# Halves of every second up-projection block made by two GpSimd transfers, with 2 raw and 3 low buffers

## The chip, the core and the metric

The kernel runs on one core of one Trainium2 chip. The engines that appear here are PE (TensorE, the matrix engine, with its weight loads shown apart as PEld), DVE (VectorE), ACT (ScalarE), POOL (GpSimd) and SP (SyncE, which here only issues transfers). A "queue" is the engine that issues a transfer: SP, ACT and POOL each issue some. The metric is the device time of one execution in microseconds; lower is better. The kernel before takes 1641.8 us, the median of two runs (1641.42 and 1642.17).

## The reference

One layer of a hybrid encoder works on 256 tokens of width 2048, in float32. A mixer with three branches (latent attention, a short gated convolution, attention into a memory) comes first. The change lies in the feed-forward part behind it:

```python
u = dwconv_centred(rmsnorm(x, ffn_norm) @ w_up, ffn_conv_w)
a, b = jnp.split(u, 2, axis=-1)
x = x + (jax.nn.silu(a) * b) @ w_down
```

`w_up` is 2048 x 11264 and `w_down` 5632 x 2048. A final RMSNorm follows.

## The kernel before

**Two halves for every weight.** Matrix products keep float32 accuracy by splitting each operand in two numbers of the type float32r. The first, `hi`, is the operand rounded to that type; the second, `lo`, is what the rounding lost. A product is then hi times both halves of the activations (512 columns: 256 tokens, high half and low half side by side) plus lo times the high half (256 columns). Weights come from HBM as float32 in blocks of 128 partitions x 2048 (1 MiB), and each block is split on the chip, in three steps:

- `load` (L129): SP issues a transfer of the block into a tile `raw`.
- `halves` (L138): ACT copies `raw` into `hi`, which rounds it.
- `halves` (L139): DVE subtracts, `lo = raw - hi`.

`block` is `load` and then `halves`. The pools have three `raw` buffers, three `hi` and two `lo`.

**Blocks on PE.** `mm` makes one output tile from one block, by `acc`: 15 products with hi (L161), 16 with lo (L163), and the last one with hi (L165). PE goes through the program block by block, about 290 of them.

**Up-projection.** `up(c)` takes two blocks, number 2c for the part `a` and 2c + 1 for the part `b`, both by `block`. Behind the products, `total` adds the two halves of a result (ACT L185, DVE L187), and DVE and ACT apply the norm's factor (L681), the convolution's three taps (L544, L545, L548) and the gate (L686, L687), and split the result f (L194, L195). There are 44 calls, in two groups: 23 before the first down-projection, which takes 32 blocks of 128 x 1408, and 21 before the second, which takes 24 such blocks and a last stage with row-major weights.

**Order.** A scheduler orders the instructions of each engine when the program is built; the order is then fixed, and each engine works its list in order, waiting at semaphores. A transfer into a tile waits until the last reader of the buffer's earlier tile is done. POOL does almost nothing in the up-projection: its one instruction there is the power in `norm_factor` (L228).

Of the kernel before, what the change touches and what calls it, by code (L numbers as in the profile page):

```python
# [12 lines left out]
F32R = mybir.dt.float32r  # L13
I32 = mybir.dt.int32
AF = mybir.ActivationFunctionType
ALU = mybir.AluOpType
# [3 lines left out]
P = 128  # L20
# [16 lines left out]
WB = 2048  # L37
# [39 lines left out]
def tile_kernel(ctx: ExitStack, tc: tile.TileContext, a, out):  # L77
    nc = tc.nc
    ctx.enter_context(nc.allow_low_precision(reason="float32r halves hold float32 exactly"))
    const = ctx.enter_context(tc.tile_pool(name="const", bufs=1))  # L80
    raws = ctx.enter_context(tc.tile_pool(name="raws", bufs=3))
    his = ctx.enter_context(tc.tile_pool(name="his", bufs=3))
    los = ctx.enter_context(tc.tile_pool(name="los", bufs=2))
    slots = ctx.enter_context(tc.tile_pool(name="slots", bufs=54))
    tmp = ctx.enter_context(tc.tile_pool(name="tmp", bufs=2))
    tiny = ctx.enter_context(tc.tile_pool(name="tiny", bufs=2))
# [3 lines left out]
    def f32(ap):  # L90
        return ap.bitcast(F32)
# [4 lines left out]
    def half(t, i):  # L96
        return t[:, i * T : (i + 1) * T]

    def temp(name):
        tag, bufs = {"hl": ("hl", 2), "t": ("t", 3), "s": ("s", 2), "sq": ("sq", 3)}.get(name, ("w", 8))  # L100
        return tmp.tile([P, T], F32, tag=tag, name=name, bufs=bufs)
# [22 lines left out]
    def load(src, n=WB, pieces=1):  # L124
        raw = raws.tile([P, WB], F32, tag="raw", name="raw")
        w = n // pieces
        for i in range(pieces):
            s = slice(i * w, (i + 1) * w)
            nc.sync.dma_start(raw[:, s], src[:, s])  # L129
            yield raw  # L130

    def halves(raw, n=WB, pieces=1):
        hi = his.tile([P, WB], F32R, tag="hi", name="hi")
        lo = los.tile([P, WB], F32R, tag="lo", name="lo")
        w = n // pieces
        for i in range(pieces):
            s = slice(i * w, (i + 1) * w)
            nc.scalar.activation(hi[:, s], raw[:, s], AF.Copy)  # L138
            nc.vector.tensor_tensor(lo[:, s], raw[:, s], f32(hi[:, s]), op=ALU.subtract)  # L139
        return hi, lo  # L140

    def block(src, n=WB, pieces=1):
        for raw in load(src, n, pieces):
            pass
        return halves(raw, n, pieces)


    def psum(pool=mmps, tag="mm"):
        return pool.tile([P, 2 * T], F32, tag=tag, name="ps")

    def mm(hi, lo, off, xs):
        ps = psum()
        acc(ps, hi, lo, off, xs, True, True)
        return ps

    def acc(ps, hi, lo, off, xs, first, final):
        n = len(xs)
        ks = [slice(off + k * P, off + (k + 1) * P) for k in range(n)]
        whole = n - 1 if final else n
        for k in range(whole):  # L160
            nc.tensor.matmul(ps, hi[:, ks[k]], xs[k], start=first and k == 0, stop=False)  # L161
        for k in range(n):
            nc.tensor.matmul(ps[:, 0:T], lo[:, ks[k]], xs[k][:, 0:T], start=False, stop=False)  # L163
        for k in range(whole, n):
            nc.tensor.matmul(ps, hi[:, ks[k]], xs[k], start=False, stop=True)  # L165
# [70 lines left out]
    def spread(r, dst=None):  # L236

        ps = atps.tile([P, 2 * T], F32, tag="at", name="pss")
        for h in range(2):
            dg = tmp.tile([P, P], F32, tag="dg", name="dg")  # L240
            nc.vector.tensor_scalar(dg, ident, r[:, h : h + 1], None, op0=ALU.mult)
            nc.tensor.matmul(ps[:, h * P : (h + 1) * P], ones, dg, start=True, stop=True)
        if dst is None:
            return ps[:, 0:T]
        nc.scalar.activation(dst, ps[:, 0:T], AF.Copy)
        return dst
# [26 lines left out]
    def wblock(pieces=1):  # L273
        return block(a["win"][next(win)], pieces=pieces)
# [24 lines left out]
    for b in range(4):  # L299
        raw = wl[b] if b < 3 else next(load(a["wkv"][b]))  # L300
        hi, lo = halves(raw, pieces=4)
# [92 lines left out]
    for unit, parts in ((TWO_PI * STEP, COARSE), (TWO_PI, FINE)):  # L394
        n = temp("n")
# [121 lines left out]
    ps = psum()  # L517
# [6 lines left out]
    for i in range(8):  # L524
        qx.append(scaled(total(mm(*wblock(), 0, xs)), rsb, f"qx{i}", XD**-0.5))
        if i == 0:
# [5 lines left out]
            ps = atps.tile([P, 2 * T], F32, tag="at", name="psk")  # L532
# [98 lines left out]
    for pair in range(KC // 2):  # L631
        ms_ = [None, None]
        for br, (w, src) in enumerate((("woa", oa), ("woc", yc), ("wom", om))):
            gs = []
            for j in range(2):
                hi, lo = wblock()
# [5 lines left out]
            hi, lo = block(a[w][pair])  # L642
# [13 lines left out]
    h2 = []  # L656
    fsq = temp("sq")
    for i in range(KC):
        if i % 2 == 0:
            nc.sync.dma_start(x2[i // 2], a["xT"][:, i * T : (i + 2) * T])  # L660
        hi, lo = block(a["wo"][i])
# [9 lines left out]
    rfb = []  # L671

    def up(c):
        ps = [mm(*block(a["wup"][2 * c + part]), 0, h2) for part in range(2)]
        if not rfb:
            rfb.append(spread(norm_factor(fsq, D, "f"), half(fb, 0)))
        ab = []
        for part in range(2):
            t = total(ps[part])
            u = temp(f"u{part}")  # L680
            nc.vector.tensor_tensor(u, t, rfb[0], op=ALU.mult)  # L681
            v = temp(f"v{part}")
            conv(u, v, "fcw", part * NFF + c, 2 * NFF)
            ab.append(v)
        s = temp("si")
        nc.scalar.activation(s, ab[0], AF.Silu)  # L686
        nc.vector.tensor_tensor(s, s, ab[1], op=ALU.mult)  # L687
        f = slot(f"f{c}", F32R)
        split(f, s)
        return f  # L690
# [29 lines left out]
    for h in range(2):  # L720
        pt = atps.tile([P, 2 * T], F32, tag="at", name="ptr")
        for c in range(TAIL):
            src = half(x2[(KC - TAIL + c) // 2], c % 2)
# [47 lines left out]
    for b in range(0, GF, 4):  # L771
        raw = raws.tile([P, WB], F32, tag="raw", name="raw")
        n = min(4, GF - b)
        for j in range(n // 2):
            nc.sync.dma_start(raw[:, j * 1024 : (j + 1) * 1024], a["wdt"][b // 2 + j])
        if b + 8 <= GF:
            hi, lo = halves(raw)
            hls = [tuple(t[:, k * 512 : (k + 1) * 512] for t in (hi, lo)) for k in range(4)]
        else:
            hls = [(slot("wh", F32R), slot("wl", F32R)) for _ in range(n)]  # L780
            for k, (hi, lo) in enumerate(hls):
                src = raw[:, k * 512 : (k + 1) * 512]
# [126 lines left out]
```

## Time and profile before

| | |
|---|---|
| median of two runs | 1641.8 us |
| the profiled execution's own time | 1642.26 us |
| its span, first to last instruction | 1640.5 us |
| PE busy in the span | 1626.7 us |
| granted TensorE clock, mean | 0.999 |
| DVE, ACT, POOL busy | 1135.0, 840.0, 11.6 us |
| read from HBM | 304.17 MB |

The span is the first table to read against: 1.8 us of the execution lie outside it. PE is busy for all but 13.8 us of the span (1640.5 - 1626.7), so what the other engines do costs time only where it makes PE wait. A busy share of an engine that is never waited for says nothing of time. The prediction quotes the lines that carry this.

### The profile page before, as it was taken

To read this page: it belongs to the slowest core of one execution; us is meant where nothing else is said; L and a number is where in the kernel's file an instruction comes from. 1 tells how busy PE (TensorE), PEld (TensorE's weight loads), DVE (VectorE), ACT (ScalarE), POOL (GpSimd) and SP (SyncE) were. 2 spreads that over 40 slices of the span, in tenths; PEclk is the share of its full clock that TensorE was granted. 3 is DMA by queue.
4 is the path that set the end of the run, shared out by engine and by line. 5 is a ranking of instruction groups with operands and counts; after the bars stand their busy time and mean duration, and the time that the engine had idled before them with its cause. 6 is when DMAs were issued, how large, how long until landed. Compare 5 with 4: busy or idle time off the path is not lost.

```text
span 1640.5 us, 23631 instructions
## 1 busy us (share of the span) xinstructions
PE 1626.7 (99%) x9626; PEld 1447.5 (88%) x9626; DVE 1135.0 (69%) x1535; ACT 840.0 (51%) x1118; POOL 11.6 (1%) x23
## 2 busy tenths in 40 slices
PE   9999999999999999999999999999999999999997
PEld 8998888998888888888888888888888888888886
DVE  7756768776666666666676777778555778777554
ACT  8634545554544544444455655555444455554552
POOL 0000000000000000000000000000000000000000
PEclk9999999999999999999999999999999999999999
DMA  8555445444555455555465555554556555554563
GB/s 319 205 187 183 169 149 199 155 160 170 184 186 199 180 192 193 180 194 191 178 234 205 181 197 187 182 199 160 179 192 210 198 196 181 194 190 161 184 213 116
DMA packets 52443, 308.97 MB, mean 188 GB/s; under 512 B 6000, under 2 KB 7536, under 8 KB 22256
## 3 DMA queue, kind: packets, MB, share of 16 engines
q1 hardware_dynamic: 50688, 305.82, 52.1%
q8 instruction: 76, 1.25, 0.3%
q10 hardware_dynamic: 1008, 1.12, 0.2%
q0 software_dynamic: 640, 0.52, 0.2%
q14 instruction: 31, 0.25, 0.0%
HBM read 304.17 MB, written 2.10 MB: 187 GB/s over the span
## 4 chain that ended last, share of the span: by engine, by line
PE 98%; DMA 1%; DVE 1%; issue 0%; ACTq 0%; ACT 0%; SPq 0%; POOLq 0%; POOL 0%; DVEq 0%
PE ps L161 51%; PE ps L163 29%; PE ps L165 4%; PE ps L173 2%; PE ps L174 2%; PE ps L175 2%; PE ps L371 1%; PE ps L372 1%; PE ps L370 1%; PE pss L436 1%; PE ps L734 0%; PE ps L736 0%; PE ps L735 0%; DMA raw<-in_wkv 0%; PE pst L460 0%
## 5 line engine op out<-in xcount | busy, mean ns | idle before, releaser
L139 DVE TENSOR_TENSOR lo<-raw,hi 128x2048 fp32r<-128x2048 f32 (+2 forms) x312 | 649.3, 2083 | 346.0 <-PE ps L163 272.1
L161 PE MATMUL ps<-h,hi 128*128 128x512 f32 x2520 | 606.5, 391 | 2.1 <-DVE t L187 2.1
L138 ACT ACTIVATE hi<-raw 128x2048 fp32r<-128x2048 f32 (+2 forms) x312 | 543.1, 1743 | 63.4 <-PE ps L175 18.2
L161 PEld LDWEIGHTS ps<-h,hi 128*128 128x128 f32 x2520 | 471.4, 188 | 96.5 <-DVE t L187 2.3
L163 PEld LDWEIGHTS ps<-h,lo 128*128 128x128 f32 x2688 | 345.0, 191 | 13.0
L163 PE MATMUL ps<-h,lo 128*128 128x256 f32 x2688 | 350.2, 283 | 0.0
L185 ACT ACTIVATE hl<-ps 128x256 f32<-128x256 f32 x253 | 97.5, 385 | 432.9 <-PE ps L165 425.8
L161 PE MATMUL ps<-f,hi 128*128 128x512 f32 x588 | 144.0, 391 | 0.0
L161 PEld LDWEIGHTS ps<-f,hi 128*128 128x128 f32 x588 | 108.6, 188 | 20.8
L187 DVE TENSOR_TENSOR t<-ps,hl 128x256 f32<-128x256 f32 x253 | 105.8, 418 | 8.7 <-ACT hl L185 8.7
L163 PEld LDWEIGHTS ps<-f,lo 128*128 128x128 f32 x616 | 81.4, 191 | 4.4
L163 PE MATMUL ps<-f,lo 128*128 128x256 f32 x616 | 82.8, 282 | 0.0
L544 ACT ACTIVATE v<-u,taps 128x256 f32<-128x256 f32 x88 | 44.7, 510 | 70.5 <-DVE u L681 70.5
L545 DVE SCALAR_TENSOR_TENSOR v<-u,taps,v 128x255 f32<-128x255 f32 x88 | 42.5, 484 | 48.8 <-ACT v L544 48.8
L165 PE MATMUL ps<-h,hi 128*128 128x512 f32 x168 | 66.6, 396 | 0.0
L161 PE MATMUL ps<-mg,hi 128*128 128x512 f32 x240 | 57.3, 390 | 0.0
L161 PEld LDWEIGHTS ps<-mg,hi 128*128 128x128 f32 x240 | 45.1, 188 | 9.1
L194 ACT ACTIVATE f<-si 128x256 fp32r<-128x256 f32 x44 | 18.3, 417 | 53.7 <-DVE si L687 53.7
L548 DVE SCALAR_TENSOR_TENSOR v<-u,taps,v 128x255 f32<-128x255 f32 x88 | 42.5, 484 | 3.0
L681 DVE TENSOR_TENSOR u<-t,fb 128x256 f32<-128x256 f32 x88 | 37.3, 425 | 2.9
L174 PE MATMUL ps<-m,lo 128*128 128x256 f32 x128 | 35.9, 284 | 0.0
L175 PE MATMUL ps<-m,hi 128*128 128x256 f32 x128 | 35.9, 284 | 0.0
(247 smaller groups left out, 1635.5 us busy)
## 6 DMA issues: line engine op xcount, KB each, us to landing
raw<-in_wup SPq DMA_DIRECT2D x88, 1024.0 KB, 4.8
raw<-in_win SPq DMA_DIRECT2D x83, 1024.0 KB, 4.8
raw<-in_wdn SPq DMA_DIRECT2D x56, 704.0 KB, 4.0
raw<-in_wo SPq DMA_DIRECT2D x16, 1024.0 KB, 4.8
raw<-in_wmk SPq DMA_DIRECT2D x8, 1024.0 KB, 4.9
raw<-in_wmv SPq DMA_DIRECT2D x8, 1024.0 KB, 4.8
raw<-in_woa SPq DMA_DIRECT2D x8, 1024.0 KB, 4.8
raw<-in_woc SPq DMA_DIRECT2D x8, 1024.0 KB, 4.7
```

The lines of the kernel that those rows point to most:

```text
L138: nc.scalar.activation(hi[:, s], raw[:, s], AF.Copy)
L139: nc.vector.tensor_tensor(lo[:, s], raw[:, s], f32(hi[:, s]), op=ALU.subtract)
L161: nc.tensor.matmul(ps, hi[:, ks[k]], xs[k], start=first and k == 0, stop=False)
L163: nc.tensor.matmul(ps[:, 0:T], lo[:, ks[k]], xs[k][:, 0:T], start=False, stop=False)
L165: nc.tensor.matmul(ps, hi[:, ks[k]], xs[k], start=False, stop=True)
L174: nc.tensor.matmul(p1, lo[:, s], x[:, 0:T], start=False, stop=False)
L175: nc.tensor.matmul(p1, hi[:, s], x[:, T:], start=False, stop=stop)
L185: nc.scalar.activation(hl, ps[:, T:], AF.Copy)
L187: nc.vector.tensor_tensor(t, ps[:, 0:T], hl, op=ALU.add)
L544: nc.scalar.activation(dst, x, AF.Copy, scale=col(w, wn + wi))
L545: nc.vector.scalar_tensor_tensor(dst[:, 1:T], x[:, 0 : T - 1], col(w, wi), dst[:, 1:T], op0=ALU.mult, op1=ALU.add)
L548: nc.vector.scalar_tensor_tensor(dst[:, 0 : T - 1], x[:, 1:T], col(w, 2 * wn + wi), dst[:, 0 : T - 1], op0=ALU.mult, op1=ALU.add,)
```

## The change

Of the two blocks of each `up(c)`, the second (the part `b`) is now made by a new function, `summed`, in place of `block`. It uses no `raw` tile and neither SP nor DVE. POOL issues a transfer of the block from HBM straight into `hi`, whose type float32r makes the transfer round (L146). ACT writes `lo = -hi` (L147). POOL then issues a second transfer of the same block from HBM that adds what it reads to what stands in `lo` (L148), so that `lo` ends as the block minus `hi`. The pools become two `raw` buffers in place of three and three `lo` in place of two.

```diff
-    raws = ctx.enter_context(tc.tile_pool(name="raws", bufs=3))
+    raws = ctx.enter_context(tc.tile_pool(name="raws", bufs=2))
     his = ctx.enter_context(tc.tile_pool(name="his", bufs=3))
-    los = ctx.enter_context(tc.tile_pool(name="los", bufs=2))
+    los = ctx.enter_context(tc.tile_pool(name="los", bufs=3))
...
+    def summed(src, n=WB):
+
+        hi = his.tile([P, WB], F32R, tag="hi", name="hi")
+        lo = los.tile([P, WB], F32R, tag="lo", name="lo")
+        nc.gpsimd.dma_start(hi[:, 0:n], src[:, 0:n])
+        nc.scalar.activation(lo[:, 0:n], f32(hi[:, 0:n]), AF.Copy, scale=-1.0)
+        nc.gpsimd.dma_start(lo[:, 0:n], src[:, 0:n], accum_op=ALU.add)
+        return hi, lo
...
-        ps = [mm(*block(a["wup"][2 * c + part]), 0, h2) for part in range(2)]
+        ps = [mm(*(block, summed)[part](a["wup"][2 * c + part]), 0, h2) for part in range(2)]
```

The lines behind `halves` move down by nine: the products with hi are L170 and L174 now, those with lo L172.

The scheduler orders the lists anew. In the rows below, a name such as hi_12320 is one tile; a block's hi, lo and product tile (ps) have numbers close together.

On POOL, the whole list of the kernel before from the rotary queries to the end is this:

```order
L602 DMA qr3_2508<-ql_2500 64x256 x2
L228 TENSOR_TENSOR fr_8679<-fe_8674,mhalf_92 128x2
L749 TENSOR_TENSOR or_15157<-om_15154,mhalf_92 128x1
L749 TENSOR_TENSOR or_15213<-om_15210,mhalf_92 128x1
L901 UNCONDITIONAL_BRANCH
```

Now 88 transfers stand between the second row and the ones before and behind it. In the first group of up-projections they come in fours, two rounding transfers and then the two adding ones:

```order
L146 DMA hi_9371<-in_wup 128x2048
L146 DMA hi_9474<-in_wup 128x2048
L148 DMA lo_9372<-in_wup 128x2048
L148 DMA lo_9475<-in_wup 128x2048
L146 DMA hi_9577<-in_wup 128x2048
L146 DMA hi_9680<-in_wup 128x2048
L148 DMA lo_9578<-in_wup 128x2048
L148 DMA lo_9681<-in_wup 128x2048
```

In the second group a block's adding transfer follows its rounding one directly:

```order
L146 DMA hi_12423<-in_wup 128x2048
L148 DMA lo_12424<-in_wup 128x2048
L146 DMA hi_12526<-in_wup 128x2048
L148 DMA lo_12527<-in_wup 128x2048
L146 DMA hi_12629<-in_wup 128x2048
L148 DMA lo_12630<-in_wup 128x2048
```

What moved in from nowhere is a chain of transfers in one list: each adding transfer waits for ACT's negation, and what stands behind it in the list waits with it.

On ACT, one call of `up` in the second group before (hi from raw twice, L138):

```order
L138 ACTIVATE hi_12933<-raw_12931 128x2048
L544 ACTIVATE v1_12817<-u1_12815,taps_84 128x256
L686 ACTIVATE si_12821<-v0_12807 128x256
L194 ACTIVATE f30_12824<-si_12821 128x256
L185 ACTIVATE hl_12905<-ps_12833 128x256
L138 ACTIVATE hi_12972<-raw_12970 128x2048
```

and now:

```order
L138 ACTIVATE hi_12901<-raw_12899 128x2048
L553 ACTIVATE v1_12786<-u1_12784,taps_84 128x256
L695 ACTIVATE si_12790<-v0_12776 128x256
L194 ACTIVATE hl_12873<-ps_12802 128x256
L553 ACTIVATE v0_12879<-u0_12877,taps_84 128x256
L203 ACTIVATE f30_12793<-si_12790 128x256
L147 ACTIVATE lo_12939<-hi_12938 128x2048
```

The second hi from raw is gone, and the negation (L147) stands in its place; it waits for the rounding transfer.

On PE, before, a block's 15 + 16 + 1 products stand together. Now the products of two blocks interleave: behind the 15 hi products of a block made by `summed` (hi_12320) come nine of the next plain block (hi_12386), and only then the lo products of the first (lo_12321):

```order
L170 MATMUL ps_12325<-h2_14_8539,hi_12320 128x512
L170 MATMUL ps_12390<-h2_0_7834,hi_12386 128x512
...
L170 MATMUL ps_12390<-h2_8_8236,hi_12386 128x512
L172 MATMUL ps_12325<-h2_0_7834,lo_12321 128x256
...
L172 MATMUL ps_12325<-h2_15_8589,lo_12321 128x256
L174 MATMUL ps_12325<-h2_15_8589,hi_12320 128x512
L170 MATMUL ps_12390<-h2_9_8286,hi_12386 128x512
```

So in the second group a low half is used later than its block's high half, by nine products. In the first group it is later still. There a round takes two calls of `up`, with the blocks A and B made by `summed`: A's hi products, a whole plain block, B's hi products, 14 products of the next plain block, A's lo, B's lo, and the rest of that plain block. In every other round A's lo stands directly behind B's hi, then 11 products of the plain block, then B's lo.

## The prediction

> **What bounds the kernel now.** I read the page's first part and the chain that ended last, then the busy times of the two up-projection groups, then one call of `up` in order of time, and last the transfers.
>
> ```profile
> PE 1626.7 (99%) x9626; PEld 1447.5 (88%) x9626; DVE 1135.0 (69%) x1535; ACT 840.0 (51%) x1118; POOL 11.6 (1%) x23
> PE 98%; DMA 1%; DVE 1%; issue 0%; ACTq 0%; ACT 0%; SPq 0%; POOLq 0%; POOL 0%; DVEq 0%
> core 0: us, PE busy (x) PEld busy (x) DVE busy (x) ACT busy (x) POOL busy (x), PEclk, DMA share, GB/s
> 870.60:1126.00 255.40, 255.40 (x1473) 225.82 (x1473) 197.42 (x271) 140.93 (x184) 0.71 (x1) 1.00 0.53 191
> 1250.00:1484.00 234.00, 234.00 (x1345) 206.72 (x1345) 177.20 (x234) 125.28 (x158) 0.00 (x0) 1.00 0.54 195
> ```
>
> The chain is PE's list. In both stretches of up-projection PE is busy all of the time at full clock, so no work of DVE there is waited for. The change takes nothing from PE's list. Even with every idle moment of PE gone the span would be 1626.7 us, 0.8% less. So there is nothing to win, and the question is whether the new chain of transfers keeps up. The pace that it must keep:
>
> ```profile
> 1000.95 0.40 PE L165 MATMUL ps<-h,hi 128*128 128x512 f32 x1
> 1001.15 2.29 DVE L139 TENSOR_TENSOR lo<-raw,hi 128x2048 fp32r<-128x2048 f32 x1 [0.37 <-PE ps L163]
> 1001.18 3.58 PE L161 MATMUL ps<-h,hi 128*128 128x512 f32 x15
> 1001.66 1.91 ACT L138 ACTIVATE hi<-raw 128x2048 fp32r<-128x2048 f32 x1
> 1004.60 2.08 PE L163 MATMUL ps<-h,lo 128*128 128x256 f32 x16
> 1006.51 0.40 PE L165 MATMUL ps<-h,hi 128*128 128x512 f32 x1
> 1006.75 3.58 PE L161 MATMUL ps<-h,hi 128*128 128x512 f32 x15
> 1007.01 0.39 ACT L185 ACTIVATE hl<-ps 128x256 f32<-128x256 f32 x1 [1.90 <-PE ps L165]
> 1012.08 0.40 PE L165 MATMUL ps<-h,hi 128*128 128x512 f32 x1
> ```
>
> From L165 to L165 a block takes 5.56 us, and two take 11.13. Fifteen products with hi take 3.42 (1001.18 to 1004.60), so one takes 0.228; the 16 with lo and the last with hi take 2.15 (1004.60 to 1006.75).
>
> **Prices of the new transfers.** The first two lines are from the page, the next two from the transfers of 870 to 1125 us, the rest from the issues and from the instructions on the tile ql.
>
> ```profile
> q1 hardware_dynamic: 50688, 305.82, 52.1%
> q0 software_dynamic: 640, 0.52, 0.2%
> ...
> q1 hardware_dynamic: 6907, 48.72, 53.0%
> raw<-in_wup SPq DMA_DIRECT2D x45, 1024.0 KB, 4.8
> ...
> raw<-in_wdn SPq DMA_DIRECT2D x56, 704.0 KB, 4.0
> sw<-qr ACTq DMA_DIRECT2D x8, 64.0 KB, 3.4
> qr<-ql POOLq DMA_DIRECT2D x8, 64.0 KB, 4.3
> ...
> L602 POOL DMA_DIRECT2D qr<-ql x8: 509/517/687, 243.8 to 256.7; - x8
> ```
>
> All 16 engines were occupied for 53.0% of 255 us by 48.72 MB, 2.77 us per MB, so a block (1.05 MB) needs 2.9 us of them. SP's transfer of a block lands 4.8 us after issue, 1.9 of which is not moving bytes.
>
> No transfer of 1 MiB issued by POOL stands in the trace. *Rounding transfer:* with 64 KB, POOL's landed in 4.3 us and ACT's in 3.4, so POOL adds 0.9; low end 4.8 + 0.9 = 5.7. High end: if rows set the time, 128 rows cost twice the 4.3 of 64 rows, 8.6. I take 5.7, since SP's row has the same bytes and shape. *Adding transfer:* it must read the block from HBM, read lo, and write lo. Low end 5.7, if the second read hides; high end 17.2, twice the 8.6. I take 5.7 + 2.9 = 8.6, a second read of 1.05 MB at the engines' rate, which is near the low end but counts bytes that must move. *Negation:* 1.91, the row of L138 with the same shape, and 0.1 for each of two waits (L185 starts 0.1 us behind the product that it waits for, 1006.91 to 1007.01).
>
> In "Collectives: The Full Stack", under "The bandwidth ceiling: the fold count and why AG ≠ RS ≠ AR", the Trainium skill says that an add in a transfer costs its engine no time of its own, but a second source read on the same ring, which halves the rate. By that rule the sum is the one below; by the low end of the rows it is the first rival's. No run here shows it yet.
>
> **The second group, 21 calls.** PE's order is 15 hi products of the summed block (3.42), nine of the next plain one (2.05), lo of the summed one (2.15), and the plain one's rest (3.5). POOL's list is hi, lo, hi, lo. A rounding transfer waits for its hi buffer, free two blocks ahead, which alone would leave 11.13 + 5.47 = 16.6 us until lo is wanted. One chain alone needs 5.7 + 2.1 + 8.6 = 16.4. But POOL's transfers follow each other on one queue, and the next rounding transfer stands behind this adding one. So from one rounding transfer's first byte to the next one's there are: 2.9 to move it, 1.9 to land, 2.1 for the negation, 0.9 for POOL to issue the adding transfer, 5.8 to move it: 13.6 us, against PE's 11.13. SP still loads the plain block through the same engines, 2.9 us per call. Where it meets POOL's transfers it delays them: between 0 and 2.9, and I take half, 1.5. The loop is 15.1, PE waits 4.0 us per call, and 21 calls cost 83 us.
>
> In "DMA: Bandwidth & Descriptors", under "Issuing engines are not separate DMA queues", the Trainium skill states that transfers of SP, ACT and POOL run on the same 16 engines and interleave. By it the 1.5 stands; with engines of POOL's own the loop would be 13.6 and this group 52 us. The profile's shares, counted over 16 engines for q0 and q1 alike, agree with it as far as they go.
>
> **The first group, 23 calls in 11.5 rounds of 22.25 us.** Counted from a round's start, when the last plain block ends: B's rounding transfer is issued at 0, moves until 3.8 and lands at 5.7. A's adding transfer, second on the queue, moves from 3.8 to 9.6 and lands at 11.5; A's lo is wanted at 12.4 at the earliest (3.42 + 5.56 + 3.42). B's negation ends at 7.8, its adding transfer moves from 9.6 to 15.4 and lands at 17.3. B's lo is wanted at 12.4 + 2.15 + 11 x 0.228 = 17.1 or, in the other rounds, 12.4 + 14 x 0.228 + 2.15 = 17.7: on time without SP's loads. These are two per round, 5.8 us; half of it meets POOL's: 2.9 us per round, 33 us in all.
>
> **The rest of the sum.**
>
> ```profile
> 8.54 1.41 SPq L129 DMA_DIRECT2D raw<-in_wkv  x2
> 14.89 0.33 SPq L129 DMA_DIRECT2D raw<-in_wkv  x1
> 16.30 0.96 SPq L129 DMA_DIRECT2D raw<-in_win  x2
> ...
> 23.45 2.19 ACT L138 ACTIVATE hi<-raw 128x512 fp32r<-128x512 f32 x4 [1.41 <-DMA raw<-in_wkv]
> ...
> 9.22 0.69 DVE L139 TENSOR_TENSOR lo<-raw,hi 128x512 fp32r<-128x512 f32 x1
> 14.97 1.29 DVE L139 TENSOR_TENSOR lo<-raw,hi 128x512 fp32r<-128x512 f32 x2
> 19.96 1.29 DVE L139 TENSOR_TENSOR lo<-raw,hi 128x512 fp32r<-128x512 f32 x2
> ```
>
> *Start.* With two raw buffers the third block's load waits for DVE to end with the first (9.22 + 0.69 = 9.9, issued at 8.54 before), the fourth's for the second (16.3, was 14.89), the fifth's for the third (21.3, was 16.30). ACT already waited 1.41 us for the fourth, so its 1.4 shows on PE. The fifth is 5.0 later with some slack. Between 1.4 and 4.7; I take 3.
>
> *Other stages.* Plain blocks have one raw buffer less and one lo buffer more, so DVE subtracts one block earlier and frees raw that much earlier; the lead is the same. What gets shorter is the loop of two raw buffers. It is closest in the down-projection:
>
> ```profile
> 1166.58 0.40 PE L165 MATMUL ps<-f,hi 128*128 128x512 f32 x1
> 1174.25 0.40 PE L165 MATMUL ps<-f,hi 128*128 128x512 f32 x1
> ...
> L139 DVE TENSOR_TENSOR lo<-raw,hi 128x1408 fp32r<-128x1408 f32 x56 | 90.9, 1625 | 85.2 <-PE ps L163 63.8 <-ACT hi L138 21.4
> L138 ACT ACTIVATE hi<-raw 128x1408 fp32r<-128x1408 f32 x56 | 76.9, 1374 | 16.5 <-PE ps L161 15.8 <-DMA raw<-in_wdn 0.7
> ...
> DMA to landing us min/median/max: 3.8/4.0/6.1
> ```
>
> Load 4.0, hi 1.37, lo 1.62 and 0.1 for SP make 7.1 us, against PE's 7.67 for two blocks (1166.58 to 1174.25). With up to 0.8 for other work ahead of it on ACT and DVE, 7.9: between 0 and 0.25 us in each of 28 pairs, 0 to 7. I take 1. A full block's loop is 4.8 + 0.1 + 1.91 + 2.29 = 9.1 against 11.13.
>
> *Removed.* 44 subtractions on DVE (44 x 2.29 = 101 us busy) and 44 loads on SP: worth nothing, as PE's unbroken 255.40 and 234.00 us cover them. ACT exchanges a rounding for a negation. Behind a negation that waits stand ACT's hl and hi of the next plain block; that hi is wanted 3.4 us into the next call, and delays with the same chain, so it is not counted again. The power fr (0.7 us on POOL) now stands behind the second rounding transfer, whose wait ends ahead of the sum that fr needs anyway: 0.
>
> The sum, against the profiled execution's 1642.3 us (0.5 above the median): 83 + 33 + 3 + 1 = 120, so 1762 us.
>
> With no meeting of SP's loads it is 52 + 0 + 4, 1698. With the rounding transfer at 8.6, the loop is 18.0 (6.9 x 21 = 144), B's lo lands 5.75 late in a round (66), and it is 1856.
>
> **Rivals.** *The second read hides* (not slower). Adding then costs 5.7, the loop is 12.2, 1.1 us over PE's pace at 21 calls or less, and the first group is on time: 1646 to 1669 us, within 2%. For it speaks that the engines were idle 47% of these stretches; against it, that POOL's loop has no slack even then (10.7 without SP's share). It decides from an adding transfer of about 7 us.
>
> *Adding is far slower per byte.* At 11.5 us (a third portion of 2.9) the loop is 18.0, and B's lo lands 8.6 late per round: 144 + 99 + 4, 1889 us. At 17.2 the loop is 23.7 (264 us) and a round 20 late (230): 2140. Nothing in the trace shows an add in a transfer, so only that absence speaks for it.
>
> *The third raw buffer is what costs.* With landings at the 6.1 us maximum the down loop is 9.2, 1.5 us over in 28 pairs: 43 us and 3 at the start, 1688 alone, with hidden adding up to 1710. Against it: 4.0 is the median.
>
> **Numbers.** Chances: the forecast 0.52, the hidden read 0.22, slow adding 0.20, raw buffers 0.05, and 0.01 for a gain that nothing here explains. A measurement of this kernel tells about 2%, 33 us, from no change. The forecast, slow adding and the raw buffers are beyond it: slower 0.77; the hidden read is within: same 0.22; faster 0.01. The likeliest time is 1762. The range reaches down to 1650, into the hidden read (0.04 below, and the 0.01), and up to 1900, which leaves out two thirds of slow adding (0.14).
>
> **What would show it.** In the profile after, L147's row should be 1.9 us on ACT, and DVE 101 us less busy. The issues of L146 and L148 give landings: 5.7 and 8.6 unhindered, some more where SP's loads meet them. PE should wait at the first lo product (L172) of summed blocks, for DMA, about 4 us per call in the second group and 3 per round in the first, and hardly at L170. Landings of L148 near 6 and a full PE would prove the first rival; above 11 the second; waits at L138 or L139 for raw in the down-projection the third. I would be wrong altogether if POOL takes several us to issue one of these transfers, since the loop then has a term that I put at 0.9.

## The result: 1776.7 us, 8.2% slower

| | before | changed |
|---|---|---|
| median of two runs | 1641.8 us | 1776.7 us (1773.65 and 1779.65) |
| the profiled execution | 1642.26 us | 1779.65 us |
| its span | 1640.5 us | 1777.9 us |
| granted TensorE clock, mean | 0.999 | 0.975 |
| read from HBM | 304.17 MB | 350.30 MB |

The time is 1.0821 times the time before, with a 95% interval from 1.0742 to 1.0901. The prediction was 1762 us with a range from 1650 to 1900, and slower as the likeliest outcome.

The page of the changed kernel: busy times, the PE slices, the transfer queues (packets, MB, share of the 16 engines), the groups that answer to the prediction (busy, mean ns of one, idle time before them and its releaser), and the issues (KB each, median us to landing).

```profile
PE 1672.9 (94%) x9626; PEld 1477.2 (83%) x9626; DVE 1027.0 (58%) x1491; ACT 824.0 (46%) x1118; POOL 72.6 (4%) x111
PE   9999998999999999999999999989998877788997
q1 hardware_dynamic: 44352, 259.68, 40.7%
q0 software_dynamic: 13312, 92.81, 20.6%
L172 PE MATMUL ps<-h,lo 128*128 128x256 f32 x2688 | 378.8, 296 | 80.9 <-DMA lo<-in_wup 80.9
L147 ACT ACTIVATE lo<-hi 128x2048 fp32r<-128x2048 f32 x44 | 84.2, 1915 | 173.0 <-DMA hi<-in_wup 173.0
...
raw<-in_wup SPq DMA_DIRECT2D x44, 1024.0 KB, 8.7
hi<-in_wup POOLq DMA_DIRECT2D x44, 1024.0 KB, 7.9
lo<-in_wup POOLq DMA_DIRECT2D x44, 1024.0 KB, 10.7
```

DVE is 108 us less busy and that buys nothing. PE now waits 80.9 us at the lo products, all of it for the adding transfers. But PE is also 46 us longer busy than before (1672.9 against 1626.7) with the same 9626 products.

The busy times in the two groups of up-projection show where that is. Columns: stretch, its length, busy time of each engine, granted clock, share of the transfer engines, GB/s. First the kernel before:

```profile
894.00:1151.00 257.00, 257.00 (x1482) 227.23 (x1481) 200.32 (x277) 140.62 (x185) 0.71 (x1) 1.00 0.52 186
1274.00:1508.00 234.00, 234.00 (x1347) 206.79 (x1346) 182.51 (x249) 126.33 (x165) 0.00 (x0) 1.00 0.52 188
```

The changed kernel:

```profile
906.00:1205.00 299.00, 272.56 (x1484) 236.00 (x1483) 142.83 (x251) 137.97 (x185) 32.98 (x46) 0.96 0.85 238
1328.00:1645.00 317.00, 259.43 (x1346) 222.33 (x1345) 128.65 (x228) 121.10 (x166) 29.13 (x41) 0.93 0.72 207
```

The same products took PE 532.0 us where they took 491.0. The clock column says why: 0.96 and 0.93 where it was 1.00. So the two groups lost 84 us of idle PE and 41 us of slower PE. (These are the groups' own stretches, from their first product with h. The prediction's two stretches began 24 us early, in the stage ahead, and left out the last 24 to 26 us of each group; the rows of before say the same either way.)

One and a half calls of the second group in order of time, changed kernel (start, duration, engine, line; in brackets the wait ahead of it and what ended it):

```profile
1505.95 3.55 PE L172 MATMUL ps<-h,lo 128*128 128x256 f32 x16 [4.12 <-DMA lo<-in_wup]
1510.68 1.92 ACT L147 ACTIVATE lo<-hi 128x2048 fp32r<-128x2048 f32 x1 [6.81 <-DMA hi<-in_wup]
1512.89 0.85 POOL L148 DMA_DIRECT2D lo<-in_wup  x1 [14.02 <-ACT hl L194]
1513.70 0.60 POOL L146 DMA_DIRECT2D hi<-in_wup  x1
...
1520.77 2.17 PE L172 MATMUL ps<-h,lo 128*128 128x256 f32 x16 [1.91 <-DMA lo<-in_wup]
1526.99 1.92 ACT L147 ACTIVATE lo<-hi 128x2048 fp32r<-128x2048 f32 x1 [7.70 <-DMA hi<-in_wup]
1529.20 0.85 POOL L148 DMA_DIRECT2D lo<-in_wup  x1 [14.90 <-ACT hl L194]
```

This is the predicted loop. The adding transfer is issued at 1512.89, and PE gets its lo at 1520.77, 7.9 us later. The next rounding transfer was issued 0.8 us behind it and lands only at 1526.99, 6.2 us after the adding one, because it stands behind it on POOL's queue and shares the time with SP's loads (e5 divides the two). Then come the negation (1.92) and the next issue at 1529.20: 16.3 us for this turn. PE's wait at the lo products is what is left of it. (The bracket at L148 names ACT's hl. The negation ends at 1512.60, just ahead of the issue, and it is what makes the tile that POOL adds to.)

For the rest of the text, a group lasts from its first product with h to the end of its last, less the products of the down-projection in between.

| kernel | time | first product with h at | first group (23 calls) | second group (21 calls) |
|---|---|---|---|---|
| before | 1641.8 | 894.5 | 257.2 | 234.0 |
| changed | 1776.7 | 906.7 (+12.2) | 298.5 (+41.3) | 316.8 (+82.8) |
| e1_pools | 1655.7 | 907.8 | 257.2 | 234.0 |
| e2_oldpools | 1795.9 | 894.7 | 332.3 | 312.0 |
| e3_noadd | 1663.4 | 907.3 | 263.1 | 234.0 |
| e4_half | 1667.2 | 906.2 | 269.7 | 234.2 |
| e5_noload | 1731.0 | 906.3 | 295.4 | 271.6 |
| e6_idle | 1853.5 | 907.9 | 361.1 | 327.0 |
| e8_addonly | 1682.7 | 906.9 | 272.4 | 247.2 |
| e9_raw2 | 1650.9 | 898.0 | 257.2 | 234.0 |
| e10_pieces | 1789.2 | 908.5 | 325.6 | 296.8 |
| e11_lo3 | 1653.7 | 905.8 | 257.2 | 234.0 |
| e12_slots50 | 1644.3 | 895.9 | 257.2 | 234.0 |
| e13_pairs | 1743.0 | 906.0 | 311.4 | 268.4 |

The three differences sum to 136.3 us of the 137.4 between the two spans. Each experiment is one run; the kernel before took 1641.6 to 1644.4 us beside them, so a difference of 2 or 3 us between two kernels says little by itself.

### The profile page after: what moved, and what is told of

Read it like the earlier page. It is cut to its first block, busy times and chain, and to the rows that moved or that the text cites. A ratio compares the mean times of both kernels' runs of the same rounds, so it can differ in the third digit from the quotient of the medians.

```text
span 1777.9 us, 23611 instructions
## 1 busy us (share of the span) xinstructions
PE 1672.9 (94%) x9626; PEld 1477.2 (83%) x9626; DVE 1027.0 (58%) x1491; ACT 824.0 (46%) x1118; POOL 72.6 (4%) x111
## 3 DMA queue, kind: packets, MB, share of 16 engines
q0 software_dynamic: 13312, 92.81, 20.6%
HBM read 350.30 MB, written 2.10 MB: 198 GB/s over the span
## 5 line engine op out<-in xcount | busy, mean ns | idle before, releaser
L139 DVE TENSOR_TENSOR lo<-raw,hi 128x2048 fp32r<-128x2048 f32 (+2 forms) x268 | 548.6, 2049 | 247.6 <-ACT hi L138 246.9
L170 PE MATMUL ps<-h,hi 128*128 128x512 f32 x2520 | 612.5, 395 | 8.8 <-DVE t L213 5.7
L170 PEld LDWEIGHTS ps<-h,hi 128*128 128x128 f32 x2520 | 478.6, 191 | 108.1 <-issue 7.7
L138 ACT ACTIVATE hi<-raw 128x2048 fp32r<-128x2048 f32 (+2 forms) x268 | 459.2, 1716 | 110.6 <-DMA raw<-in_wdn 29.6
L172 PE MATMUL ps<-h,lo 128*128 128x256 f32 x2688 | 378.8, 296 | 80.9 <-DMA lo<-in_wup 80.9
L172 PEld LDWEIGHTS ps<-h,lo 128*128 128x128 f32 x2688 | 364.5, 203 | 106.4 <-DMA lo<-in_wup 95.8
L147 ACT ACTIVATE lo<-hi 128x2048 fp32r<-128x2048 f32 x44 | 84.2, 1915 | 173.0 <-DMA hi<-in_wup 173.0
L170 PE MATMUL ps<-f,hi 128*128 128x512 f32 x588 | 144.6, 392 | 0.0
L170 PEld LDWEIGHTS ps<-f,hi 128*128 128x128 f32 x588 | 108.6, 189 | 20.7
L172 PEld LDWEIGHTS ps<-f,lo 128*128 128x128 f32 x616 | 81.4, 191 | 4.4
L172 PE MATMUL ps<-f,lo 128*128 128x256 f32 x616 | 82.8, 283 | 0.0
L174 PE MATMUL ps<-h,hi 128*128 128x512 f32 x168 | 69.3, 413 | 0.0
L146 POOL DMA_DIRECT2D hi<-in_wup x44 | 28.3, 643 | 945.0 <-PE ps L174 814.3
L170 PE MATMUL ps<-mg,hi 128*128 128x512 f32 x240 | 57.3, 391 | 0.0
L148 POOL DMA_DIRECT2D lo<-in_wup x44 | 38.0, 864 | 359.1 <-ACT hl L194 270.0
L170 PEld LDWEIGHTS ps<-mg,hi 128*128 128x128 f32 x240 | 45.2, 188 | 9.0
L554 DVE SCALAR_TENSOR_TENSOR v<-u,taps,v 128x255 f32<-128x255 f32 x88 | 42.2, 481 | 12.2 <-ACT v L553 12.2
## 6 DMA issues: line engine op xcount, KB each, us to landing
lo<-in_wup POOLq DMA_DIRECT2D x44, 1024.0 KB, 10.7
```

The source lines that it names most:

```text
L146: nc.gpsimd.dma_start(hi[:, 0:n], src[:, 0:n])
L147: nc.scalar.activation(lo[:, 0:n], f32(hi[:, 0:n]), AF.Copy, scale=-1.0)
L148: nc.gpsimd.dma_start(lo[:, 0:n], src[:, 0:n], accum_op=ALU.add)
L554: nc.vector.scalar_tensor_tensor(dst[:, 1:T], x[:, 0 : T - 1], col(w, wi), dst[:, 1:T], op0=ALU.mult, op1=ALU.add)
```

## Experiments

### Which part of the change costs what

**e1_pools.** The pools alone; both blocks by `block`.

```diff
-        ps = [mm(*(block, summed)[part](a["wup"][2 * c + part]), 0, h2) for part in range(2)]
+        ps = [mm(*block(a["wup"][2 * c + part]), 0, h2) for part in range(2)]
```

> The changed kernel's pools (2 raw, 3 low) with both blocks of every call made as before; nothing is left out. The trace of the changed kernel is already 12.2 us late where the last stage ahead of the up-projection starts. If the pools and the order they lead to cost that: about 1654 us, all of the loss ahead of the up-projection, none in it. If the prediction's 4 us for the pools was right and the rest came from elsewhere: about 1646. If the 12.2 were chance of that one execution: 1642.

Measured: 1655.7 us. Both groups last as before, and all of the loss, 13.3 us, lies ahead of the up-projection. So the changed kernel's 12.2 us there are not the new transfers' doing.

**e2_oldpools.** The transfers alone, with the old pools.

```diff
-    raws = ctx.enter_context(tc.tile_pool(name="raws", bufs=2))
+    raws = ctx.enter_context(tc.tile_pool(name="raws", bufs=3))
...
-    los = ctx.enter_context(tc.tile_pool(name="los", bufs=3))
+    los = ctx.enter_context(tc.tile_pool(name="los", bufs=2))
```

> The two transfers with the pools of before (3 raw, 2 low). The scheduler now puts the next block's rounding transfer ahead of this block's adding transfer on POOL for most of the calls. Queue theory: the negation and the landing are then covered by the other block's transfer, the queue needs 2.9 + 5.8 us and up to 2.9 of SP's per call, 8.7 to 11.6 against PE's 11.13, so PE waits 0 to 1 us per call in the second group in place of 4, and the stages ahead cost nothing: 1645 to 1690 us. Rival, the length of the adding transfer itself (10.7 us to land) sets the wait whatever the order: the second group stays 80 us late, 1760 or more.

Measured: 1795.9 us, and the expectation failed. The early loss is gone, but the first group is 34 us worse than in the changed kernel. The waits of this run (engine, tile, line, what it waited for: us in total, times, longest) tell why:

```profile
POOL hi L146 <- PE ps L174: 380.7, 37, 17.5
DVE lo L139 <- PE ps L172: 303.3, 150, 10.2
ACT lo L147 <- PE ps L172: 167.6, 27, 9.3
```

With two low buffers the negation has to wait until PE is done with an earlier lo, 27 times and up to 9.3 us, and what stands behind it on ACT and on POOL's queue waits with it. In the first group, then, the two transfers need the third low buffer, which costs elsewhere. The second group is 5 us shorter without it.

**e9_raw2, e11_lo3, e12_slots50.** These three divide e1's 13 us. All three are the kernel before with other pools: two raw buffers; three low buffers and 50 tiles of the slots pool; the 50 tiles alone.

```diff
-    raws = ctx.enter_context(tc.tile_pool(name="raws", bufs=3))
+    raws = ctx.enter_context(tc.tile_pool(name="raws", bufs=2))
```

```diff
-    los = ctx.enter_context(tc.tile_pool(name="los", bufs=2))
-    slots = ctx.enter_context(tc.tile_pool(name="slots", bufs=54))
+    los = ctx.enter_context(tc.tile_pool(name="los", bufs=3))
+    slots = ctx.enter_context(tc.tile_pool(name="slots", bufs=50))
```

> The kernel before with two raw buffers and its own two low buffers, both blocks loaded as before. It asks which pool costs the 12 to 14 us ahead of the up-projection, which the changed pools alone showed too. If the third raw buffer is what is missed, the mark of the first gate product comes about 12 us later than before and the total is 1652 to 1658. If the third low buffer moves the order of the list instead, the total is 1641 to 1645.

> The kernel before with three raw and three low buffers; for the room the slots pool has 50 tiles and not 54. Two raw buffers with two low ones cost 3.5 us ahead of the up-projection, two raw with three low 13.3. If the third low buffer's order of the list costs the other 10, the first gate product comes 8 to 13 us later than in the kernel before (805.5); if it takes both pools together, it comes within 3 us of it. Whether the 50 slots have a part in it, the run beside it tells.

> The kernel before with 50 tiles in the slots pool and nothing else, for comparison with the run with three low buffers: 1641 to 1650 if the slots aren't scarce there.

Measured: the first product with h comes 3.5 us later with two raw buffers, 11.3 with three low ones, 1.4 with the 50 slots alone. So the third low buffer costs about 9.9, and two raw buffers 3.5, together 13.4; e1 shows 13.3. Of the 3.5 us, only 2.1 are the raw buffer's: the other 1.4 e12 has too, at the same products, with three raw buffers. The 2.1 arise at one wait, in products with the memory, where before PE goes on without a pause (e9_raw2):

```profile
68.25 0.39 PE L174 MATMUL ps<-m,lo 128*128 128x256 f32 x1 [1.79 <-DVE lo L139]
```

The total of e9, 1650.9 us, lies between its two expectations (1641 to 1645, 1652 to 1658). The low buffer costs through the order: with it the scheduler's list has a place where PE has nothing to do. Three times PE's order of time, with the wait in brackets. First e11_lo3:

```profile
271.81 5.50 PE L161 MATMUL ps<-h,hi 128*128 128x512 f32 x15 [5.55 <-DVE t L204]
```

The changed kernel:

```profile
271.85 6.29 PE L170 MATMUL ps<-h,hi 128*128 128x512 f32 x15 [5.08 <-DVE t L213]
```

And the longest wait of the kernel before, earlier in its list:

```profile
231.84 3.70 PE L161 MATMUL ps<-h,hi 128*128 128x512 f32 x15 [2.05 <-DVE t L187]
```

A wait of 5.1 to 5.6 us, and then 15 products that take 5.5 to 6.3 us and not 3.6: against the row of before, some 5 to 6 of the 10 us are at this one place. Most of the rest, 4.5 us, is lost at 86 to 90 us, at two waits of 1.5 us. e9_raw2 also loses about 5 us behind the up-projection, in the last stage; with three low buffers that loss is absent.

### Is it the second read of the adding transfer?

**e3_noadd.** The second transfer writes the block over lo and adds nothing.

```diff
-        nc.gpsimd.dma_start(lo[:, 0:n], src[:, 0:n], accum_op=ALU.add)
+        nc.gpsimd.dma_start(lo[:, 0:n], src[:, 0:n])
```

> The second transfer of each block writes the block into lo and does not add (lo is then not the rounding's remainder); every list of every engine is the same as in the changed kernel. If the adding transfer costs twice a plain one, and that drives the loop: POOL's queue is occupied about 2.5 us per MB in place of 4, the loop is 10.7 to 12.2 us, PE waits 0 to 1.1 us per call in the second group and not in the first: 1655 to 1685 us with the 12 us lost ahead. If the add costs nothing extra: 1775, as the changed kernel.

Measured: 1663.4 us. The second group loses nothing, the first 6 us. The list of each engine is that of the changed kernel, and so are the 92.81 MB on POOL's queue. The share of the engines and the landings are not; this run's rows:

```profile
q0 software_dynamic: 13312, 92.81, 16.3%
...
hi<-in_wup POOLq DMA_DIRECT2D x44, 1024.0 KB, 5.2
lo<-in_wup POOLq DMA_DIRECT2D x44, 1024.0 KB, 6.7
```

16.3% of 1661.6 us is 271 us of engine time for those bytes; with adding it was 20.6% of 1777.9 us, 366 us. Without the 95 us between them the chain keeps up with PE. The kernel leaves out the adding and the reading of lo together, so it doesn't tell which of the two takes the time.

**e4_half.** Only every second call makes its second block by `summed`.

```diff
-        ps = [mm(*(block, summed)[part](a["wup"][2 * c + part]), 0, h2) for part in range(2)]
+        ps = [mm(*(block, summed)[part * (c % 2)](a["wup"][2 * c + part]), 0, h2) for part in range(2)]
```

> Only every second call of up makes its second block by the two transfers (22 blocks in place of 44). Queue theory: a loop of 15 to 16 us against 22.3 us of PE work between two such blocks, so PE waits for none of them: 1642 plus the 12 us lost ahead of the up-projection, 1650 to 1660 us. Rival, a fixed price of about 2.8 us per block made this way (124.5 us over 44): 62 us in the up-projection, about 1716.

Measured: 1667.2 us, above the 1650 to 1660 expected; a fixed price per block (1716) is out. Of the loss 11.7 us are the early loss and 12.5 lie in the first group, most of it in its first rounds. In the second group half of the blocks cost nothing at all: a chain has 22 us there and needs some 16. Its issues give the new transfers' landings (medians of both groups; in the second alone the adding ones land in 7.8 to 8.4 us):

```profile
hi<-in_wup POOLq DMA_DIRECT2D x22, 1024.0 KB, 5.2
lo<-in_wup POOLq DMA_DIRECT2D x22, 1024.0 KB, 8.7
```

### The queue or the bytes?

Both theories know the second read. By the first, what costs is that rounding, negation and adding follow each other on one queue, with the engines idle in between. By the rival, the engines are simply too slow for these bytes.

**e8_addonly.** hi is rounded by ACT from a raw tile again; negation and adding transfer stay.

```diff
-        nc.gpsimd.dma_start(hi[:, 0:n], src[:, 0:n])
+        raw = next(load(src))
+        nc.scalar.activation(hi, raw, AF.Copy)
```

> The 44 blocks keep the negation and the adding transfer, but hi is rounded by ACT from a raw tile that SP loads, as in the kernel before. Per call the 16 transfer engines then move the same 3 block reads and one reading of lo as in the changed kernel (by the two unhindered landings about 10 us of engine time against the 11.13 us of PE), but the queue of POOL holds only adding transfers, one per call, and no rounding transfer stands between two of them. Queue theory (one rounding, one negation and one adding transfer follow each other on one queue): the second group, +83 us in the changed kernel, loses 0 to 10, the first 0 to 15, the start the 13 of the two raw buffers; total 1655 to 1680. Rival (the adding transfers simply occupy the engines for too long, whatever the queue): the second group stays at +60 or more, total 1740 to 1780.

Measured: 1682.7 us. The second group loses 13.2 us and not 82.8, with the same bytes through the same engines; the queue theory expected 0 to 10, the rival 60 or more. The transfers of 1310 to 1540 us in this run:

```profile
DMA packets 8631, 62.27 MB, mean 271 GB/s; under 512 B 960, under 2 KB 960, under 8 KB 1216
q1 hardware_dynamic: 5760, 41.29, 48.5%
q0 software_dynamic: 2857, 20.78, 46.9%
```

Plain transfers took 2.70 us per MB (48.5% of 230 us by 41.29 MB), adding ones 5.19, 1.92 times as long (46.9% of 230 us by 20.78 MB). One call (two plain blocks of 1.05 MB and an adding one) is 11.1 us of engine time, just PE's 11.13. So the rest of the loss here, 0.6 us per call, may be the engines', which are at 95%; no run tests that. The changed kernel's second group had them at 72% (the column 0.72 above).

**e5_noload.** The plain blocks load their raw tile once per group instead of once per call; the adding chain stays.

```diff
-        ps = [mm(*(block, summed)[part](a["wup"][2 * c + part]), 0, h2) for part in range(2)]
+    once = []
...
+    def plain(src, n=WB, pieces=1):
+        if len(once) in (0, 23):
+            raw = next(load(src))
+        else:
+            raw = once[-1]
+        once.append(raw)
+        return halves(raw)
...
+        ps = [mm(*(plain, summed)[part](a["wup"][2 * c + part]), 0, h2) for part in range(2)]
```

> The plain blocks of the up-projection load their raw tile once per group, not once per call, and are rounded and subtracted from that one tile in each call, so the output isn't the reference's: left out are 42 of SP's 44 loads, and nothing else. In PE's list of this kernel the first group goes call by call too, as the second does in both. Queue theory with the price that the prediction gave to the meeting of SP's loads (1.5 us per call): the loop on the queue falls from 14.94 to about 13.5 us, the second group takes 21 x 13.5 = 284 us (317 in the changed kernel, 234 before), the first 23 x 13.5 = 310, total about 1655 + 50 + 54 = 1760. Rival A (the engines' total load is the bound): without 2.5 to 2.9 us of load per call the loop falls to PE's pace or near it, second group 234 to 245, total 1655 to 1680. Rival B (SP's loads hardly touch the queue of POOL): loop 14.9, second group 313, total about 1820.

Measured: 1731.0 us. The second group takes 271.6 us, 12.93 per call, where the queue theory expected 13.5 and its rivals PE's pace or 14.9. The row of the first of a series of 13 waits at lo and that of the last:

```profile
1348.55 2.17 PE L172 MATMUL ps<-h,lo 128*128 128x256 f32 x16 [1.96 <-DMA lo<-in_wup]
...
1500.97 2.18 PE L172 MATMUL ps<-h,lo 128*128 128x256 f32 x16 [1.23 <-DMA lo<-in_wup]
```

They are 12 turns apart, 12.70 us each. Without any load of SP the chain alone is still slower than PE. The transfers of 1330 to 1590 us say what the turn is made of:

```profile
q0 software_dynamic: 5788, 42.17, 64.6%
```

64.6% of 260 us by 42.17 MB is 3.98 us per MB, so the two blocks of a call are 8.4 us of engine time. The other 4.3 to 4.6 us of the turn the engines stand idle: landing, negation and issue.

Beside the changed kernel this run also shows where SP's loads hurt. In both, an adding transfer of the second group lands 7.8 to 7.9 us after its issue (medians). The rounding transfer behind it lands 4.7 us later in the changed kernel and 2.5 us later here. So the whole 2.16 us per call that SP's loads cost (15.09 - 12.93) falls on the rounding transfers.

**e6_idle.** 20 products with zeros more in each block made by `summed`, between its hi and its lo products.

```diff
+    zero = const.tile([P, T], F32R, name="zero")
...
+        for _ in range(idle):
+            nc.tensor.matmul(ps[:, 0:T], hi[:, ks[0]], zero, start=False, stop=False)
```

> Between the hi and the lo products of each of the 44 blocks PE gets 20 more products with a tile of zeros (128x256, about 2.4 us by the lo products' 2.08 for 16 at full clock), which add nothing to the sum. PE's list of this kernel takes the blocks strictly one after the other, in both groups. If the loop is the queue's and PE only waits at its end, the second group doesn't change (317 us, period 14.9), PE's wait for lo falls from about 4 to 1 to 2 us, and the granted clock comes back to near 1.0, so that the 16 lo products take 2.1 us and not 3.6; the first group, call by call now, takes 23 x 14.9 = 344; total about 1820. Rival: PE's work and its halved clock behind a wait are a part of the loop; then 44 x 2.4 = 105 us come on top, or, if the clock was the loss, the second group gets shorter than 317 by up to 21 x 1.5 = 31 us.

Measured: 1853.5 us. PE got 52 us more to do in the second group (21 x 2.5), and the group became 10 us longer. Four fifths of the work fit into the waits, so PE is mostly off the loop, but not wholly: 15.6 us per call against 15.1. (PE's list isn't the changed kernel's either: the blocks stand one after the other, so the 52 us aren't the only difference.) Two rows show the way back from PE to the queue:

```profile
1515.41 3.78 PE L177 MATMUL ps<-h,lo 128*128 128x256 f32 x16 [3.38 <-DMA lo<-in_wup]
...
1526.12 0.55 POOL L149 DMA_DIRECT2D hi<-in_wup  x1 [3.26 <-PE ps L179]
```

A wait of 3.4 us is followed by lo products that take 1.7 times as long, and the next rounding transfer then waits 3.3 us for the hi buffer that PE has yet to free. The clock wasn't held at 1.00 as expected, but came to 0.95, and the first group, call by call in this list, took 361 us and not 344.

**e13_pairs.** An activation of 256 columns more per block on ACT, overwritten at once. It moves the list: the second group now goes in rounds of two calls too, with two rounding transfers and then two adding ones on the queue.

```diff
+        nc.scalar.activation(lo[:, 0:256], f32(hi[:, 0:256]), AF.Copy, scale=-1.0)
         nc.scalar.activation(lo[:, 0:n], f32(hi[:, 0:n]), AF.Copy, scale=-1.0)
```

> The changed kernel with a small activation more per block on ACT (256 columns of lo, overwritten at once by the negation; about 0.4 us by the rows of that width). By it the list of the second group comes out in rounds of two calls too, as in the first: two rounding transfers on the queue, then two adding ones, and no negation between a rounding and the next rounding. Queue theory (what counts is what stands between two transfers on the queue): the second group goes at the pace of the first, 12.98 us per call, 21 x 12.98 = 273 us instead of 317, total 1730 to 1745. Rival (the bytes set the pace, so the order on the queue doesn't matter): second group 310 to 325, total 1775 to 1790.

Measured: 1743.0 us, and the second group 268.4 us, 48 less than in the changed kernel, with more work and the same bytes. Behind two rounding transfers the first block's negation runs while the second transfer still moves; it lands at 1444.35. ACT in order of time:

```profile
1439.37 1.92 ACT L148 ACTIVATE lo<-hi 128x2048 fp32r<-128x2048 f32 x1
...
1444.35 0.42 ACT L147 ACTIVATE lo<-hi 128x256 fp32r<-128x256 f32 x1 [1.51 <-DMA hi<-in_wup]
1444.79 1.92 ACT L148 ACTIVATE lo<-hi 128x2048 fp32r<-128x2048 f32 x1
```

The order on the queue matters, then, and the rival (310 to 325) is out. The queue isn't all of this turn, though: behind the first two, every rounding transfer waits 4 to 12 us for PE to free a hi buffer ahead of its issue. The first group's list differs somewhat as well, and it took 13 us more than in the changed kernel, so this isn't the order alone in both groups. It is the fastest kernel here that makes all 44 blocks by both transfers and leaves nothing out, and still 6% behind the kernel before.

**e10_pieces.** Each of the two transfers in two pieces of 1024 columns, so that one piece is negated while the other moves.

```diff
-        nc.gpsimd.dma_start(hi[:, 0:n], src[:, 0:n])
-        nc.scalar.activation(lo[:, 0:n], f32(hi[:, 0:n]), AF.Copy, scale=-1.0)
-        nc.gpsimd.dma_start(lo[:, 0:n], src[:, 0:n], accum_op=ALU.add)
+        parts = [slice(0, n // 2), slice(n // 2, n)]
+        for p in parts:
+            nc.gpsimd.dma_start(hi[:, p], src[:, p])
+        for p in parts:
+            nc.scalar.activation(lo[:, p], f32(hi[:, p]), AF.Copy, scale=-1.0)
+            nc.gpsimd.dma_start(lo[:, p], src[:, p], accum_op=ALU.add)
```

> The changed kernel with each block from the two new transfers cut into two pieces of 1024 columns: two rounding transfers, then for each piece its negation and its adding transfer. The bytes are the same, the issues on POOL twice as many. Queue theory: of the 12.7 us that one call takes on the queue without SP's loads, 8.4 are bytes and 4.3 are landing, negation and issue in series with the engines idle; in pieces the second rounding piece moves while the first is negated, which hides 1.5 to 2.5 of it. The second group falls from 317 to 265 to 285 us, total 1690 to 1735. Rival (the rate of the adding transfers and of SP's loads together sets the loop, not the gap): second group 310 to 325, total 1770 to 1800.

Measured: 1789.2 us, outside what the queue theory expected. The second group gained 20 us and not 32 to 52, and the first lost 27. Two things changed besides. The rows of 4 KB cost more: 60.5% of the 300 us from 1340 to 1640 by 41.94 MB, 4.33 us per MB, was 3.96 in the changed kernel (54.1% of the same stretch by 41.02 MB):

```profile
q0 software_dynamic: 11516, 41.94, 60.5%
```

Second, POOL's list became irregular, with up to four adding pieces in a row. So this run doesn't tell how much of the 4.3 idle us pieces could hide.

## Why the prediction was right

**What bounds the kernel.** PE at 99% had nothing to win, and the removed work of DVE (101 us predicted, 108 measured) bought nothing. The new wait is at the lo products, for the adding transfer, as predicted.

**Prices.** Rounding 5.7 predicted, 5.2 measured where nothing hinders it; adding 8.6 and 8.7 (e4's median), but 7.8 in the changed kernel's second group, where the price was used; negation 1.91 and 1.915; POOL's issue 0.9 and 0.85 to 0.9. The one open price, the second read, was taken as a second plain read of engine time, and e8's rows say the same: 5.19 against 2.70 us per MB. The Trainium skill's "Collectives: The Full Stack", "The bandwidth ceiling: the fold count and why AG ≠ RS ≠ AR", says of the reducing step of a collective that its second source read halves the rate. The trace agrees in size, 1.92 times as long. That the time goes into a second read, and not into the adding itself, no run separates. e3, which takes both away and leaves everything else, shows that it decides.

**Second group.** Predicted a loop of 15.1 us and 83 us in all; measured 15.09 per call (316.8 / 21) and 82.8. Two terms of it were each off by 0.7, in opposite directions. The loop without SP's loads was put at 13.6 and is 12.93 in e5, since the adding transfer lands in 7.9 us there and not in 8.6; the meeting with SP's loads was put at 1.5 and is 15.09 - 12.93 = 2.16. "I take half" was too little: three quarters of SP's 2.9 us land on the chain, all of it on the rounding transfer. So a part of the close agreement is luck.

**First group.** Predicted 33, measured 41.3: 3.6 us per round of two calls and not 2.9. Which term was mis-sized stays open. One candidate is half of SP's 5.8 us per round: with the share that the second group shows, three quarters, it would be 4.3. The other is a term that the prediction put at nothing. Of the 41.3 us, 26.4 are idle PE (299 - 272.56) and 15.6 slower products (272.56 - 257), and in this group the rounding transfers wait for PE to free a hi buffer, 5 to 10 us each:

```profile
995.05 0.55 POOL L146 DMA_DIRECT2D hi<-in_wup  x1 [10.35 <-PE ps L174]
1003.18 0.55 POOL L146 DMA_DIRECT2D hi<-in_wup  x1 [7.57 <-PE ps L174]
```

So slower products can lengthen a round here. No run keeps this group's order without SP's loads, which would tell the two apart.

**Start.** Predicted 3, measured 12.2, and this step failed. Two raw buffers alone come out at 3.5 (e9), near the 3, but that is luck. The prediction put the loss at the first five loads, within 25 us of the start; by 30 us e9 is 0.5 us late, and so is e12, which has three raw buffers. The missing buffer costs 2.1 us later, at 68.25. What the prediction missed is the third low buffer, which it met with "the lead is the same" for plain blocks. It costs 9.9 (e11 against e12), and not by a raw or low buffer that is late: a pool's size moves the scheduler's whole list, also in stages that the change doesn't touch.

**Other stages.** Predicted 1; the stretches between and behind the groups differ by 1.1 us in all.

**The rivals.** The hidden second read is out (landings of 7.8 to 8.7, PE not full); far slower adding is out (the same landings, and not 11.5 or more; the median of 10.7 in the changed kernel is that of transfers that stand behind others on the queue). The third raw buffer costs 2 to 3.5 us ahead of the up-projection, and some 5 in the last stage only where there are two low buffers, far from 43.

The sum was 120 and the profiled difference 137.4: 9 us of the gap are the low buffer's list at the start, 8 the first group.

**What was not seen at all** is the form in which the loss comes. The prediction told it as waits of PE. Of some 125 us in the two groups, 84 are waits and 41 are products at a lower clock. So it isn't only by PE's waits that the other engines cost time. The second group's total was right nevertheless, since its loop runs over the queue: what PE loses by the clock, it waits less. e6 bears that out from the other side, with four fifths of the added work hidden.

## What to carry to other kernels

An adding transfer occupied the transfer engines 1.92 times as long as a plain one here, so price it as two reads of its bytes. Then lay out its queue as a loop (rounding, landing, negation, issue, adding) and compare the turn with the pace of the engine that it feeds: here 12.9 us alone, 15.1 with other loads in the way, against 11.13, though the bytes alone come to about 11.1 (e8), just PE's pace. Order the queue so that another transfer's bytes cover each hand-over to an engine, and look at what a pool's new size does to the list in stages that the change doesn't touch.

## What the runs showed of the hardware beyond expectation

**PE can run at half its clock behind a wait of some 2 us.** The 16 lo products, which take 2.17 us behind a short wait, in the changed kernel, and last the row of 1176.90 to 1178.80 us (columns as above), with a granted clock of 0.50:

```profile
990.84 3.67 PE L172 MATMUL ps<-h,lo 128*128 128x256 f32 x16 [2.39 <-DMA lo<-in_wup]
...
1022.56 2.18 PE L172 MATMUL ps<-h,lo 128*128 128x256 f32 x16 [1.85 <-DMA lo<-in_wup]
...
1176.89 3.78 PE L172 MATMUL ps<-h,lo 128*128 128x256 f32 x16 [3.66 <-DMA lo<-in_wup]
...
1176.90:1178.80 1.90, 1.90 (x9) 1.90 (x10) 0.00 (x0) 0.00 (x0) 0.00 (x0) 0.50 0.64 244
```

The limit isn't sharp: in the changed kernel the products took 3.25 us behind a wait of 1.92 and 3.60 behind 1.96, but 2.18 behind 2.78 and 3.28. There no wait shorter than 1.9 us was followed by slower products; in e4 one of 1.74 was (2.65). In "TensorE: Matmul & The Clock Gate", "Part 1: The HAM clock gate", the Trainium skill puts the fall to half the clock behind an idle window of about 3.4 us. The halving agrees with the 0.50; the length doesn't, as here waits of 1.9 to 2.4 us were already followed by it. Since the waits table doesn't count this time, it undercounts what the waits cost: in these two groups 84 us of waits came with 41 us of slower products.

**Loads of SP and transfers of POOL slow each other.** Taking SP's loads away made the chain on POOL's queue 2.16 us per call faster, with nothing changed on that queue. SP's own loads of w_up landed in 8.7 us (median) beside the chain and in 4.8 before.
